# One weight sum of each seven-product pair made by an accumulating DMA, in a hybrid encoder block on one core

## The chip, the cores and the metric

The kernel runs on one core of a Trainium2 chip. The metric is the device time of one execution in microseconds (us). The engines are TensorE (PE; its weight loads are listed as PEld), VectorE (DVE), ScalarE (ACT), GpSimd (POOL) and SyncE (SP). SP issues the loads of the weights; GpSimd issues a few DMAs of its own.

## What is computed

One layer of a streaming encoder: a joint input projection, retention heads, latent-attention heads, an output projection, a layer norm, and a feed-forward part. The change lies in the feed-forward part, on 256 tokens:

```
x = LN(alpha * x + concat(A, B) @ W_out)          # 256 x 2048
h = square(relu(x @ W_up)) @ W_down               # W_up 2048 x 8192, W_down 8192 x 2048
x = LN(alpha * x + h)
```

All of it is float32.

## The kernel before, in words

**Products in parts.** TensorE multiplies in a rounded form of float32 (fp32r). To keep the precision, every operand is split into a high part (rounded, a ScalarE cast, L389) and a low part (operand minus high part, a VectorE subtraction, L390), and every product is three matmuls: high by high, high by low, low by high. Tokens are the stationary operand, weights the moving one, 512 columns at a time.

**Pairs.** The weights come in pairs of 128-row slices: a load of 1 MB fills a raw tile of 128 x 2048 that holds two slices of 1024 columns each. Call the slices' column halves B11, B12 (first slice) and B21, B22 (second slice), and the four token blocks of the activations x11 to x22 alike. An ordinary pair (pair_products, L1293) splits each slice once (two splits of 1024 columns, two slots) and runs 24 matmuls. A seven-product pair, or seven (seven_products, L429), uses Winograd's form of Strassen's scheme: seven products of 128 x 128 by 128 x 512 in place of eight, 21 matmuls. It needs four sums of the token blocks (token_sums, L360: four VectorE instructions L364 to L367, a ScalarE cast L368 and a VectorE subtraction L369 for the low part) and, of the weights, three sums made on VectorE in weights_pair (L371): t13 (1024 columns, L398), a new content of B12 in place (512 columns, L404), and t4 (512 columns, L408). Four splits follow: w0 (second slice), w1 (first slice), w2 (t13), w3 (t4, 512 columns).

**What sets the order.** Every pair is a Job with a load and a list of pieces. unit(), called after each group of matmuls, hands out up to two pieces (next_piece, L177) in the order of the jobs; SEVEN_PARTS gives the order within a seven: token sums s0, t13 s1, split w0, s2, w2, s3, w1, w3. Split weights live in five slots (NSLOT) of a high and a low tile; a split waits for the slot that was used five splits earlier, while sums need no slot and may be handed out ahead. Raw tiles are three (NRAW): load_ahead (L160) issues the load of a job on SP's queue when the job three ahead of it has been handed out, and on the chip it waits for that job's last reader of the raw tile.

**Up stage.** After a first part with other shapes (j_up), seven blocks b = 1 to 7 run eight pairs each over 1024 columns of W_up. UP_SEVEN makes pairs 3 and 5 of block 1 and pairs 2, 3, 5, 6 of the other six blocks sevens: 26 in all. Their token sums are made once (pair_sums). The products that belong to several outputs gather in four PSUM banks; up_gather (L1309) combines them, up_finish adds them to the block's result, which TensorE transposes.

**Down stage.** Two passes p = 0, 1 over 1024 columns of W_down each; in each pass 32 pairs at places n = 0 to 31. ORDER and TURNED give the order of the pairs, SEVEN the places that are sevens. At every even place r_split splits the next block of activations (ScalarE cast L1233, VectorE low part L1237); in pass 0, r_keep stores the low part in HBM by a GpSimd DMA (L1243), and pass 1 fetches it by a GpSimd DMA (L1235). A seven of pass 1 whose pair is in STORED = (27, 9, 22, 25, 4, 7) uses the token sums that pass 0 left in the tile sx; every other seven makes its own. add_sums (L1394) combines the gathered products after the last seven of a pass, one step per unit; in pass 1 its last step is two matmuls (L1428). The last four pairs of pass 1 are staged, their splits kept for the end. The retention stage has sevens too (half_pair, L454); they go through weights_pair as well.

Of the kernel before, what the change touches and what calls it, by code (L numbers as in the profile page):

```python
# [12 lines left out]
ALU = mybir.AluOpType  # L13

P = 128
# [22 lines left out]
SEVEN = ((4, 7, 9, 12, 14, 17, 19, 22, 25, 27), (2, 4, 6, 8, 10, 12, 14, 16, 18, 20, 22))  # L38
# [5 lines left out]
SEVEN_PARTS = ('s0', 's1', 'w0', 's2', 'w2', 's3', 'w1', 'w3')  # L44
X1_AT = ((1, 2), 1)
# [47 lines left out]
class Job:  # L93


    def __init__(self, load, pieces, slotted):
        self.load = load
        self.pieces = pieces
        self.slotted = slotted
        self.slots = None  # L100
        self.left = None
        self.seven = False
        self.held = False
# [8 lines left out]
def kernel(  # L112
# [45 lines left out]
    state = {"dma": 0, "job": 0, "unit": 0, "pause": 0, "heads": 0}  # L158
# [202 lines left out]
    def token_sums(r0, r1, st, v):  # L361
# [4 lines left out]
        nc.vector.tensor_sub(st[:, 2], r0[:, 0:P], r0[:, P:])  # L366
# [4 lines left out]
    def weights_pair(name, load, half, columns, sums=None, seven=False, into=None):  # L371
# [24 lines left out]
        def first():  # L396
            a, b, t13 = columns(job, extra["t13"])
            nc.vector.tensor_sub(t13, a, b)  # L398
            if sums:
                job.rest()  # L400
# [8 lines left out]

        job.load = lambda: load(job)  # L410
        job.seven = seven
        if not seven:
            job.pieces = [lambda e=e: split(e, half(job, e, 0, 8)) for e in range(2)]
            job.slots = [e if into is None or into[e] is None else None for e in range(2)]
        else:
            parts = {"s0": token_part, "s1": first, "s2": second, "s3": third,
                     "w0": lambda: split(0, half(job, 1, 0, 8)), "w1": lambda: split(1, half(job, 0, 0, 8)),
                     "w2": lambda: split(2, extra["t13"]), "w3": lambda: split(3, extra["t4"], 512)}
            job.pieces = [parts[p] for p in SEVEN_PARTS]
            job.slots = [int(p[1]) if p[0] == "w" else None for p in SEVEN_PARTS]  # L420
# [8 lines left out]
    def seven_products(job, x, k, sums, cb, mb, first, last, done=None):  # L429
        for a, w, o, pb, alone in ((("x", 1, 0), 0, 0, cb[0][0], False), (("s", 3), 0, 512, cb[0][1], False),  # L430
                                   (("s", 0), 2, 0, mb[2], True), (("s", 2), 2, 512, mb[3], True),
                                   (("x", 0, 0), 1, 0, mb[0], True), (("s", 1), 1, 512, mb[1], True),
                                   (("x", 1, 1), 3, 0, cb[1][0], False)):
# [110 lines left out]
    def up_pair(b, kp):  # L544
        def load(job):
            raw = raw_tile(job, f"raw_wu{b}_{kp}")
            nc.sync.dma_start(raw.rearrange("p (f c) -> p f c", f=8),
                              w_up[8 * b:8 * b + 8, :, kp * 256:(kp + 1) * 256].rearrange("f p c -> p f c"))

# [3 lines left out]
        def columns(job, t):  # L553
            v = job.raw.rearrange("p (f e c) -> p f e c", f=8, e=2)
            return (v[:, 4:8].rearrange("p f e c -> p e f c"), v[:, :, 0].rearrange("p (j f) c -> p j f c", j=2),
                    t.rearrange("p (j f c) -> p j f c", j=2, c=P))

        return weights_pair(f"wu{b}_{kp}", load, half, columns, None, kp in UP_SEVEN[b])

    def down_pair(p, pair, into=None, seven=None):  # L560
        def load(job):
            raw = raw_tile(job, f"raw_wd{p}_{pair}")
            nc.sync.dma_start(raw.rearrange("p (e c) -> p e c", e=2),
                              w_down[2 * pair:2 * pair + 2, :, p * 1024:(p + 1) * 1024].rearrange("e p c -> p e c"))

# [9 lines left out]
        def columns(job, t):  # L575
            return (job.raw.rearrange("p (e j c) -> p e j c", e=2, j=2)[:, :, 1],
                    job.raw[:, 0:1024].rearrange("p (j c) -> p j c", j=2), t.rearrange("p (j c) -> p j c", j=2))

        return weights_pair(f"wd{p}_{pair}", load, half, columns, None if seven is None or p == 1 and pair in STORED else sums, seven is not None, into)
# [729 lines left out]
    def up_gather(mb):  # L1309
# [10 lines left out]
        nc.vector.tensor_add(g[1], g[1], g[3])  # L1320
        yield
        nc.vector.tensor_add(g[3], g[3], g[2])
# [73 lines left out]
    def add_sums(p, mb):  # L1396
# [14 lines left out]
        nc.vector.tensor_add(v, v, p5)  # L1411
        yield
        plus(1, 1, v)
        nc.vector.tensor_add(u, u, p5)
# [195 lines left out]
```

## Time and profile before

| | |
|---|---|
| median of 3 runs | 1100.75 us (1100.7 to 1100.85) |
| the profiled execution | 1100.88 us |
| its span, first to last instruction | 1099.1 us |
| granted TensorE clock | 0.999 |
| POOL busy | 24.7 us, 46 instructions |
| DMA | 231.78 MB, mean 211 GB/s |
| up blocks 1 to 7 / down passes, in the span | to about 754 us / to about 1090 us |

The span is what the profiler records from the first to the last instruction; the time of the execution has 1.8 us more around it. A row of instructions reads: start in us, duration, engine, line, operation, destination <- sources, shapes, count, and in brackets the idle time before it with what ended it. A row grouped by line ends in: busy us in total, mean ns of one, idle us before them. A DMA row gives the size of one transfer and the median time from its issue to its landing. "PE d L353" is a matmul into a tile called d issued from line 353, the line of the ordinary pairs; L441 is that of the sevens.

### The profile page before, as it was taken

What the parts mean: (1) busy time and instruction counts of PE and PEld (TensorE: products, weight loads), DVE (VectorE), ACT (ScalarE), POOL (GpSimd) and SP (SyncE); (2) the same over time, 40 slices, a digit from 0 to 9 for tenths busy, and PEclk for the clock granted to TensorE, in tenths of its full rate; (3) what the DMA queues carried; (4) which work ended last, traced back from release to release, by engine and by line L of the source; (5) the groups of instructions that cost most, each with busy time, mean ns of one, the idle gap of its engine ahead of it and who ended that gap; (6) DMA issues with size and microseconds to landing.
All of it is one profiled execution on the core that took longest, in us unless ns stands there. A gap on an engine that the chain in (4) does not pass through costs nothing.

```text
span 1099.1 us, 13768 instructions
## 1 busy us (share of the span) xinstructions
PE 1091.1 (99%) x5145; PEld 912.1 (83%) x5145; DVE 955.4 (87%) x1304; ACT 656.7 (60%) x847; POOL 24.7 (2%) x46
## 2 busy tenths in 40 slices
PE   9999999999999999999999999999999999999997
PEld 8888888888888889888888888888888888888885
DVE  7878779889785777889999999999899999999985
ACT  4545556546463455467777677776666663666660
POOL 0000000000000000000000000000000000000000
PEclk9999999999999999999999999999999999999999
DMA  8655364535266544666656756757677876777792
GB/s 286 243 201 188 138 225 171 222 115 208 109 230 230 216 176 154 194 200 197 213 171 196 234 165 192 230 181 271 205 249 253 260 239 220 264 238 263 255 336 97
DMA packets 97026, 231.78 MB, mean 211 GB/s; under 512 B 4672, under 2 KB 63040, under 8 KB 89152
## 3 DMA queue, kind: packets, MB, share of 16 engines
q1 hardware_dynamic: 92496, 215.64, 57.6%
q0 software_dynamic: 4032, 14.68, 3.9%
q8 instruction: 40, 0.66, 0.2%
q10 hardware_dynamic: 432, 0.59, 0.2%
q14 instruction: 26, 0.21, 0.1%
HBM read 221.46 MB, written 9.44 MB: 210 GB/s over the span
## 4 chain that ended last, share of the span: by engine, by line
PE 97%; DVE 1%; DMA 1%; issue 0%; ACT 0%; POOL 0%; SPq 0%; DVEq 0%
PE d L353 21%; PE u L353 15%; PE r L353 12%; PE o L353 8%; PE v L441 6%; PE s L441 5%; PE u L441 5%; PE m L353 5%; PE d L441 4%; PE rs L441 2%; PE up L924 2%; PE pu L924 2%; PE r L441 1%; PE ut L1353 1%; PE pv L353 1%; PE up L930 1%
## 5 line engine op out<-in xcount | busy, mean ns | idle before, releaser
L353 PE MATMUL d<-hi_wd,rhl 128*128 128x512 f32 x632 | 174.7, 390 | 0.0
L390 DVE TENSOR_TENSOR lo_wd<-raw_wd,hi_wd 128x1024 fp32r<-128x1024 f32 x125 | 150.4, 1220 | 19.9 <-ACT hi_wd L389 19.5
L389 ACT CAST hi_wd<-raw_wd 128x1024 fp32r<-128x1024 f32 x125 | 129.3, 1051 | 56.1 <-DVE raw_wd L404 17.8
L390 DVE TENSOR_TENSOR lo_wu<-raw_wu,hi_wu 128x1024 fp32r<-128x1024 f32 x112 | 135.5, 1220 | 12.0 <-ACT hi_wu L389 10.9
L353 PEld LDWEIGHTS d<-hi_wd,rhl 128*128 128x128 f32 x632 | 118.4, 188 | 24.3
L389 ACT CAST hi_wu<-raw_wu 128x1024 fp32r<-128x1024 f32 x112 | 117.7, 1055 | 34.5 <-PE u L353 10.6
L353 PE MATMUL u<-hi_wu,x1hl 128*128 128x512 f32 x480 | 137.0, 394 | 0.0
L353 PE MATMUL r<-hi_ret,xhl 128*128 128x512 f32 x384 | 110.2, 397 | 0.0
L353 PEld LDWEIGHTS u<-hi_wu,x1hl 128*128 128x128 f32 x480 | 88.3, 188 | 17.2
L353 PE MATMUL d<-lo_wd,rhl 128*128 128x512 f32 x316 | 97.7, 389 | 0.0
L353 PEld LDWEIGHTS r<-hi_ret,xhl 128*128 128x128 f32 x384 | 71.0, 188 | 14.1
L390 DVE TENSOR_TENSOR lo_ret<-raw_ret,hi_ret 128x1024 fp32r<-128x1024 f32 x64 | 76.1, 1218 | 6.9 <-ACT hi_ret L389 6.7
L389 ACT CAST hi_ret<-raw_ret 128x1024 fp32r<-128x1024 f32 x64 | 65.9, 1052 | 25.6 <-PE r L353 14.7
L353 PE MATMUL u<-lo_wu,x1hl 128*128 128x512 f32 x240 | 74.2, 390 | 0.0
L353 PEld LDWEIGHTS d<-lo_wd,rhl 128*128 128x128 f32 x316 | 59.3, 188 | 12.4
L353 PE MATMUL r<-lo_ret,xhl 128*128 128x512 f32 x192 | 59.5, 391 | 0.0
L353 PE MATMUL o<-hi_wo,mix 128*128 128x512 f32 x208 | 57.5, 393 | 0.0
L441 PE MATMUL v<-hi_wu,us 128*128 128x512 f32 x156 | 56.5, 389 | 0.0
L353 PEld LDWEIGHTS u<-lo_wu,x1hl 128*128 128x128 f32 x240 | 45.0, 188 | 9.6
L441 PE MATMUL s<-hi_wd,sx 128*128 128x512 f32 x126 | 45.6, 389 | 0.0
L353 PEld LDWEIGHTS o<-hi_wo,mix 128*128 128x128 f32 x208 | 38.7, 188 | 7.8
L240 ACT CAST hi_wo<-raw_wo 128x1024 fp32r<-128x1024 f32 x26 | 27.0, 1054 | 27.4 <-PE o L353 19.1
(341 smaller groups left out, 2210.6 us busy)
## 6 DMA issues: line engine op xcount, KB each, us to landing
raw_wu<-in_w_up SPq DMA_DIRECT2D x64, 1024.0 KB, 5.4
raw_wd<-in_w_down SPq DMA_DIRECT2D x64, 1024.0 KB, 5.9
raw_ret<-in_w_ret SPq DMA_DIRECT2D x32, 1024.0 KB, 4.8
raw_wo<-in_w_out SPq DMA_DIRECT2D x16, 1024.0 KB, 4.8
raw_mla<-in_w_mla SPq DMA_DIRECT2D x14, 672.0 KB, 5.1
lo_kept<-rhl POOLq DMA_DIRECT2D x14, 512.0 KB, 4.1
rhl<-lo_kept POOLq DMA_DIRECT2D x13, 512.0 KB, 3.6
raw_qk<-in_w_qk SPq DMA_DIRECT2D x8, 640.0 KB, 3.9
```

Of the source, the lines that this page charges most:

```text
L240: nc.scalar.copy(hi[:, o:e], r)
L353: nc.tensor.matmul(accs[j][:, :w], x_part, w_part[:, a:a + w], start=first and fst and i == 0, stop=last and lst and i == len(steps) - 1)
L389: nc.scalar.copy(h, src)
L390: nc.vector.tensor_sub(l, src, h.bitcast(F32))
L441: nc.tensor.matmul(pb, x_part, w_part, start=alone and first and fst, stop=alone and last and lst)
L924: nc.tensor.matmul(pb, hi[:, a:a + P], hl[:, k0 + i], start=first and i == ks[0], stop=last and i == ks[-1])
L930: nc.tensor.matmul(pb[:, 0:S], lo[:, a:a + P], hl[:, k0 + i, 0:S], start=False, stop=last and i == ks[-1])
L1353: nc.tensor.transpose(pts[i][:, f * P:(f + 1) * P], gathered[i][:, f * P:(f + 1) * P], ident)
```

## The change

In the up and down stages (not in retention), a seven is made in a new way. After the load of its raw tile, GpSimd issues a DMA that reads the first half of the first slice (B11) from HBM once more and adds it to the second half (B12) in the raw tile: 512 rows of 512 bytes in the up stage, 128 rows of 2 KB in the down stage, 256 KB each. add_ahead issues it, from next_piece, once the job before it is being handed out. VectorE then makes t4 = (B11 + B12) - B22 (512 columns) and t13 = [B11, B21] - t4 (1024 columns, t4 read twice). The order within a seven becomes s0, s2, s3, w0, w1, w2, w3 (ADDED_PARTS), the low part of the token sums follows t4, and the seven products run in another order over the four splits. Some sums have the opposite sign, so the third token sum and the combinations in up_gather and add_sums change signs. The places of the sevens in the down passes become 4, 6, 8, 11, 13, 16, 18, 21, 23, 25, 27 (eleven, ten before) and 3, 5, ..., 23 (eleven, as before at 2, 4, ..., 22). STORED, TURNED, UP_SEVEN, NRAW and NSLOT stay as they are.

```diff
-SEVEN = ((4, 7, 9, 12, 14, 17, 19, 22, 25, 27), (2, 4, 6, 8, 10, 12, 14, 16, 18, 20, 22))
+SEVEN = ((4, 6, 8, 11, 13, 16, 18, 21, 23, 25, 27), (3, 5, 7, 9, 11, 13, 15, 17, 19, 21, 23))
...
 SEVEN_PARTS = ('s0', 's1', 'w0', 's2', 'w2', 's3', 'w1', 'w3')
+ADDED_PARTS = ('s0', 's2', 's3', 'w0', 'w1', 'w2', 'w3')
...
+    def add_ahead():
+        while state["added"] and jobs.index(state["added"][0][0]) <= state["job"] + 1:
+            _, dst, src = state["added"].pop(0)
+            nc.gpsimd.dma_start(dst, src, accum_op=ALU.add)
...
         load_ahead(state["job"])
+        add_ahead()
...
-        nc.vector.tensor_sub(st[:, 2], r0[:, 0:P], r0[:, P:])
+        nc.vector.tensor_sub(st[:, 2], r0[:, P:], r0[:, 0:P])
...
             nc.vector.tensor_sub(t13, a, b)
-            if sums:
-                job.rest()
...
+        def added_second():
+            b22 = half(job, 1, 4, 8)
+            nc.vector.tensor_sub(shaped(extra["t4"], b22), half(job, 0, 4, 8), b22)
+            if sums:
+                job.rest()
+
+        def added_third():
+            low = columns(job)
+            t4, t13 = extra["t4"], extra["t13"].rearrange("p (e c) -> p e c", e=2)
...
+            nc.vector.tensor_sub(t13, low, t4.unsqueeze(1).to_broadcast(low.shape))
...
+        if job.plus:
+            steps = ((("x", 1, 0), 0, 0, cb[0][0], False), (("s", 3), 0, 512, cb[0][1], False),
+                     (("x", 0, 0), 1, 0, mb[0], True), (("s", 0), 1, 512, mb[2], True),
+                     (("s", 2), 2, 0, mb[3], True), (("x", 1, 1), 2, 512, cb[1][0], False),
+                     (("s", 1), 3, 0, mb[1], True))
...
-                if done and w == 1:
+                if done and w == (3 if job.plus else 1):
                     side.append(done)
...
+            if job.seven:
+                state["added"].append((job, half(job, 0, 4, 8),
+                                       w_up[8 * b:8 * b + 4, :, kp * 256:kp * 256 + P].rearrange("f p c -> p f c")))
...
+            if job.seven:
+                state["added"].append((job, raw[:, 512:1024], w_down[2 * pair, :, p * 1024:p * 1024 + 512]))
...
-        nc.vector.tensor_add(g[1], g[1], g[3])
+        nc.vector.tensor_sub(g[1], g[3], g[1])
...
-        nc.vector.tensor_add(v, v, p5)
+        nc.vector.tensor_sub(v, p5, v)
```

More of the change, by code (lines that the diff above doesn't have):

```diff
@@ L102, in __init__ @@
         self.seven = False
+        self.plus = False
         self.held = False
@@ L157 @@
     holders = []
-    state = {"dma": 0, "job": 0, "unit": 0, "pause": 0, "heads": 0}
+    state = {"dma": 0, "job": 0, "unit": 0, "pause": 0, "heads": 0, "added": []}
     def load_ahead(upto):
@@ L369, in token_sums, with weights_pair @@
         return lambda: nc.vector.tensor_sub(v[:, :, 1], st, v[:, :, 0].bitcast(F32))
-    def weights_pair(name, load, half, columns, sums=None, seven=False, into=None):
+    def weights_pair(name, load, half, columns, sums=None, seven=False, into=None, plus=False):
         job = Job(None, [], into is None or None in into)
@@ L408, in third @@
             nc.vector.tensor_sub(shaped(extra["t4"], b21), b21, half(job, 0, 4, 8))
+        def added_second():
[6 more added lines that the diff above has]
+            t4, t13 = extra["t4"], extra["t13"].rearrange("p (e c) -> p e c", e=2)
+            if len(low.shape) == 4:
+                t4 = t4.rearrange("p (f c) -> p f c", c=P)
+                t13 = t13.rearrange("p e (f c) -> p e f c", c=P)
+            nc.vector.tensor_sub(t13, low, t4.unsqueeze(1).to_broadcast(low.shape))
         job.load = lambda: load(job)
         job.seven = seven
+        job.plus = plus
         if not seven:
@@ L415, in weights_pair @@
         else:
-            parts = {"s0": token_part, "s1": first, "s2": second, "s3": third,
+            parts = {"s0": token_part, "s1": first, "s2": added_second if plus else second,
+                     "s3": added_third if plus else third,
                      "w0": lambda: split(0, half(job, 1, 0, 8)), "w1": lambda: split(1, half(job, 0, 0, 8)),
                      "w2": lambda: split(2, extra["t13"]), "w3": lambda: split(3, extra["t4"], 512)}
-            job.pieces = [parts[p] for p in SEVEN_PARTS]
-            job.slots = [int(p[1]) if p[0] == "w" else None for p in SEVEN_PARTS]
+            names = ADDED_PARTS if plus else SEVEN_PARTS
+            job.pieces = [parts[p] for p in names]
+            job.slots = [int(p[1]) if p[0] == "w" else None for p in names]
         job.hi, job.lo = [None] * 4, [None] * 4
@@ L429, in seven_products @@
     def seven_products(job, x, k, sums, cb, mb, first, last, done=None):
[L430 to L433, printed above, removed]
+        if job.plus:
[3 more added lines that the diff above has]
+                     (("s", 1), 3, 0, mb[1], True))
+        else:
+            steps = ((("x", 1, 0), 0, 0, cb[0][0], False), (("s", 3), 0, 512, cb[0][1], False),
+                     (("s", 0), 2, 0, mb[2], True), (("s", 2), 2, 512, mb[3], True),
+                     (("x", 0, 0), 1, 0, mb[0], True), (("s", 1), 1, 512, mb[1], True),
+                     (("x", 1, 1), 3, 0, cb[1][0], False))
+        for a, w, o, pb, alone in steps:
             use_slot(job, w)
@@ L548, in load, with columns @@
                               w_up[8 * b:8 * b + 8, :, kp * 256:(kp + 1) * 256].rearrange("f p c -> p f c"))
+            if job.seven:
+                state["added"].append((job, half(job, 0, 4, 8),
+                                       w_up[8 * b:8 * b + 4, :, kp * 256:kp * 256 + P].rearrange("f p c -> p f c")))
         def half(job, e, i, j):
             return job.raw.rearrange("p (f e c) -> p f e c", f=8, e=2)[:, i:j, e]
[L553 to L558, printed above, removed]
+        def columns(job):
+            return job.raw.rearrange("p (f e c) -> p f e c", f=8, e=2)[:, 0:4].rearrange("p f e c -> p e f c")
+        return weights_pair(f"wu{b}_{kp}", load, half, columns, None, kp in UP_SEVEN[b], plus=True)
     def down_pair(p, pair, into=None, seven=None):
@@ L573, in sums, with columns @@
             return token_sums(r0, r1, st, sums_of(seven, pair))
[L575 to L579, printed above, removed]
+        def columns(job):
+            return job.raw.rearrange("p (e j c) -> p e j c", e=2, j=2)[:, :, 0]
+        return weights_pair(f"wd{p}_{pair}", load, half, columns, None if seven is None or p == 1 and pair in STORED else sums, seven is not None, into, True)
     def sums_of(q, pair):
```

4 lines of the change are left out of this document (2 added, 2 removed).

## The prediction, on record before the result

> **What bounds the kernel now.** I read the page's busy table first, then the chain of waits with its steps in order of time, then who waits for whom on the engine that carries the chain, and only then the stages.
>
> ```profile
> span 1099.1 us, 13768 instructions
> PE 1091.1 (99%) x5145; PEld 912.1 (83%) x5145; DVE 955.4 (87%) x1304; ACT 656.7 (60%) x847; POOL 24.7 (2%) x46
> ...
> PE 97%; DVE 1%; DMA 1%; issue 0%; ACT 0%; POOL 0%; SPq 0%; DVEq 0%
> ```
>
> A busy share of 99% alone proves little, since the ends of matmuls are modelled. The chain says more: 97% of the span is TensorE following itself. The next rows are the chain in order of time inside the second down pass, one ordinary pair and one seven-product pair ("a seven" from here on).
>
> ```profile
> 938.83 5.44 PE d L353 x24
> 944.27 1.36 PE d L441 x6
> 945.63 2.72 PE s L441 x12
> 948.35 0.68 PE d L441 x3
> ```
>
> A pair is 24 matmuls in 5.44 us, 226.7 ns each. A seven is 21 in 1.36 + 2.72 + 0.68 = 4.76 us, the same 226.7 ns each. So neither contains a wait. The list of TensorE's waits agrees; these are its two longest entries (us in total, times, longest), one at the start of the kernel and one in its tail:
>
> ```profile
> PE last L1513 <- ACT xm L1511: 1.5, 1, 1.5
> PE m L616 <- POOL warm L613: 1.0, 1, 1.0
> ```
>
> TensorE is therefore fed everywhere in the up and down stages, and time falls only by removing matmuls. The stages show how narrowly it is fed (columns: TensorE, weight loads, VectorE, ScalarE, GpSimd, clock, DMA share, GB/s):
>
> ```profile
> 600.00:700.00 100.00, 100.00 (x458) 82.80 (x458) 94.82 (x104) 73.04 (x90) 0.00 (x0) 1.00 0.63 199
> 800.00:900.00 100.00, 100.00 (x443) 82.84 (x442) 97.76 (x123) 64.90 (x73) 4.78 (x9) 1.00 0.75 246
> 900.00:1000.00 100.00, 100.00 (x442) 82.68 (x442) 94.20 (x111) 59.48 (x65) 3.72 (x7) 1.00 0.72 249
> ```
>
> VectorE is at 95 to 98% there. It is not the bound, but it is next, and whatever stalls it has little room.
>
> **The change, part by part.**
>
> *Matmuls.* The first down pass gets 11 sevens for 10; the second keeps 11, the up blocks 26. One pair becomes a seven: 5.44 - 4.76 = 0.68 us less on the path. The new order of the seven steps keeps 21 matmuls each and costs nothing on TensorE, as long as the operands are there.
>
> *VectorE, removed and added.* Durations of one, by line and form:
>
> ```profile
> L404 DVE TENSOR_TENSOR raw_wu<-raw_wu,t 128x512 f32<-128x512 f32 x26 | 17.9, 688 | 0.4
> L404 DVE TENSOR_TENSOR raw_wd<-raw_wd,t 128x512 f32<-128x512 f32 x21 | 14.4, 684 | 0.0
> L364 DVE TENSOR_TENSOR xm<-rr 128x128 f32<-128x128 f32 x15 | 4.3, 284 | 0.0
> L369 DVE TENSOR_TENSOR sx<-xm,sx 128x512 fp32r<-128x512 f32 x15 | 10.3, 684 | 0.0
> ```
>
> Consecutive instructions overlap a little, so I count from start to start, from this piece of the first down pass (last split of a pair, then a seven):
>
> ```profile
> 861.12 1.22 DVE L390 TENSOR_TENSOR lo_wd<-raw_wd,hi_wd 128x1024 fp32r<-128x1024 f32 x1
> 862.26 0.28 DVE L364 TENSOR_TENSOR xm<-rr 128x128 f32<-128x128 f32 x1
> ...
> 863.19 1.22 DVE L398 TENSOR_TENSOR t<-raw_wd 128x1024 f32<-128x1024 f32 x1
> 864.33 0.69 DVE L369 TENSOR_TENSOR sx<-xm,sx 128x512 fp32r<-128x512 f32 x1
> 864.93 1.22 DVE L390 TENSOR_TENSOR lo_wd<-raw_wd,hi_wd 128x1024 fp32r<-128x1024 f32 x1
> ```
>
> A 1024-wide instruction takes 1.14 us, a 512-wide one 0.60, the four token sums 0.93. Per seven, three weight instructions (1024, 512, 512) become two (512, 1024): the L404 one goes, 26 + 21 = 47 times 0.60 = 28.2 us. The eleventh seven costs 0.60 + 1.14 + 3 x 1.14 + 0.60 = 5.76 us of weight work where a pair has 2 x 1.14 = 2.28: plus 3.5. And there is a part that the title doesn't name. The second pass reuses six token sums of the first through the list STORED (pairs 27, 9, 22, 25, 4, 7), which the change leaves alone; its sevens move to odd places, that is to pairs 31, 23, 24, 26, 1, 3, 5, 6, 8, 11, 13, and none of them is in the list. So the second pass makes 11 sets of sums for 5, the first 11 for 10: 22 sets for the 15 of the rows above, 7 x (0.93 + 0.60) = 10.7 us more. Sum on VectorE: -28.2 + 3.5 + 10.7 = -14 us, all beside TensorE's work: worth nothing by itself. ScalarE gets seven more 512-wide casts and about 1.7 us for the new seven, under its 40% of idle time: nothing.
>
> *The sums by DMA.* 48 transfers of 256 KB from HBM, each added into the upper half of a weight tile in SBUF. Each waits on GpSimd's queue for the tile's own load to land; the first VectorE weight instruction of the seven, and ScalarE's cast for the second split, wait for the sum. What has to fit is load plus sum into the cover between the issue of the load and that VectorE instruction. No accumulating transfer is in this trace. Its neighbours (KB each, us to landing; then GpSimd's time for one descriptor job):
>
> ```profile
> raw_wu<-in_w_up SPq DMA_DIRECT2D x64, 1024.0 KB, 5.4
> raw_wd<-in_w_down SPq DMA_DIRECT2D x64, 1024.0 KB, 5.9
> lo_kept<-rhl POOLq DMA_DIRECT2D x14, 512.0 KB, 4.1
> rhl<-lo_kept POOLq DMA_DIRECT2D x13, 512.0 KB, 3.6
> out<-xm SPq DMA_DIRECT2D x6, 256.0 KB, 2.2
> ```
>
> ```profile
> L1243 POOL DMA_DIRECT2D lo_kept<-rhl x14 | 7.7, 547 | 469.2 <-PE u L353 344.3 <-DVE rhl L1237 124.9
> ```
>
> Low end: the 256 KB store, 2.2 us; a gain is excluded, since the transfer is added. High end: two 1 MB loads and a store that overlapped,
>
> ```profile
> raw_wd<-in_w_down SPq DMA_DIRECT2D x2, 1024.0 KB, 8.3
> ```
>
> landed 2.4 us later than the median load, so 4.1 + 2.4 = 6.5 us; in the up blocks a sum has 512 rows of 512 bytes for the 128 rows of the GpSimd row, and if that job grows fourfold from 0.547 us, 1.6 us more: 8.1. I take 3.9, the middle of the two GpSimd rows of 512 KB, because a sum moves 256 KB in and has to read and write 256 KB at its target. Load plus sum is then 9.3 us in the up blocks and 9.8 in the down passes.
>
> The Trainium skill (page Collectives: The Full Stack, section "The bandwidth ceiling: the fold count and why AG ≠ RS ≠ AR") says that an adding transfer runs at about half a copy's rate, not for the addition but because it reads two sources. By that rule a 256 KB sum costs what a 512 KB copy costs here; were it a mere copy, 2.2 us, load plus sum would be 7.6 and 8.1 us and no seven would be late. No row here shows an adding transfer, so neither is tested yet.
>
> *The cover.* Issues of the load that feeds a seven, and the instruction that will need the sum (the sevens of an up block, then of the first pass after two pairs, then of the second pass):
>
> ```profile
> 619.56 0.37 SPq L547 DMA_DIRECT2D raw_wu<-in_w_up  x1
> 628.85 1.22 DVE L398 TENSOR_TENSOR t<-raw_wu 128x1024 f32<-128x1024 f32 x1
> 856.09 0.37 SPq L563 DMA_DIRECT2D raw_wd<-in_w_down  x1
> 958.79 0.37 SPq L563 DMA_DIRECT2D raw_wd<-in_w_down  x1
> 968.88 0.28 DVE L364 TENSOR_TENSOR xm<-rr 128x128 f32<-128x128 f32 x1
> 979.87 0.28 DVE L364 TENSOR_TENSOR xm<-rr 128x128 f32<-128x128 f32 x1
> ```
>
> Up: 628.85 - 619.56 = 9.3 us, even with 9.3. First pass: 863.19 - 856.09 = 7.1; there the tile is freed by a seven's third split, and in the new order by its second, 1.14 us earlier, so 8.2 against 9.8: 1.6 us late, at the three sevens that follow two pairs. At the seven other steps, with one pair between, the load goes out at the end of the pair ahead of the seven before, and the cover is 0.93 plus a whole step of 10.7 us (below). Second pass: 968.88 + 0.93 - 958.79 = 11.0, 1.2 to spare.
>
> *Does VectorE bear the lateness?* A seven with token sums takes it 5.76 + 0.93 + 0.60 = 7.29 us. First pass, seven and pair: 7.29 + 2.28 + 1.14 (the low part of the next block's activations) = 10.71 against TensorE's 10.20, -0.5; with two pairs 7.29 + 4.56 + 1.7 = 13.6 against 15.6, +2.1, and +0.5 after the 1.6 us. Over its ten steps (places 4, 6, 8, 11, 13, 16, 18, 21, 23, 25, 27), 7 x -0.5 + 3 x 0.5 = -2. The lead that pays for it is thin now; the tightest place of this pass is the pair at
>
> ```profile
> 857.72 3.49 DVE L390 TENSOR_TENSOR lo_wd<-raw_wd,hi_wd 128x1024 fp32r<-128x1024 f32 x3
> 859.87 10.88 PE d L353 x48
> ```
>
> whose first split ends at 857.72 + 1.22 = 858.94, 0.9 us ahead of TensorE. Each seven before it now gives 0.60 back, so some 2 us of lead stand against the -2: just enough. Second pass: 7.29 + 2.28 = 9.6 against 10.2, lead grows. So nothing of the lateness reaches TensorE, by a small margin.
>
> *What else is moved.* GpSimd's queue also stores and fetches the kept low parts; a store behind a waiting sum has two blocks (20 us) until its buffer is rewritten, a fetch one block (10.2 us) for its 3.6: hidden unless a sum waits over 6 us. The combination of partial products after the last seven starts one unit later, and its two matmuls in the second pass then fall in the last unit of place 27, ahead of the staged pairs: nothing.
>
> Total: -0.68 us. The profiled execution took 1100.88 (span 1099.1 and 1.8 around it), so 1100.20; against the median of the runs, 1100.75, it is 1100.1.
>
> **Rivals.**
>
> *The sums land late* (slower). They share the 16 DMA engines with loads that fill 63 to 75% of them; 51 GB/s more in the second pass (256 KB read twice per 10.2 us) is about a sixth more. VectorE works in order, so a late sum stops splits, gathers and residuals alike. In the first pass a seven after two pairs breaks even at 2.1 us late, that is at a sum of 4.4 us, and the lead is gone near 5. In the second pass loads run two steps ahead, the step becomes (load + sum + 9.57 - 0.93)/2, and passes 10.20 at a sum of 5.9. With 6.5 us: first pass 3 x (12.4 - 8.2 + 13.6 - 15.6 = 2.1) + 7 x 0.5 less 3 of lead = 7; second 10 x 0.3 less 2 to 3 of lead, about 1; together 1108. With 8.1 the same sums give 12 and 9, 1121, and the up blocks, 4.2 us late at their first seven, come on top. For it: VectorE at 97.8%, the 8.3 us row. Against: the 3.6 and 4.1 rows were made beside that same traffic. The Trainium skill (page DMA: Bandwidth & Descriptors, section "Issuing engines are not separate DMA queues") states that transfers from any engine interleave on the same 16. The 8.3 us row agrees.
>
> *The second pass pays for its sums* (slower). Its steps with sums now take 979.87 - 968.88 = 10.99 us, with waits for ScalarE inside, such as
>
> ```profile
> 978.73 1.23 DVE L390 TENSOR_TENSOR lo_wd<-raw_wd,hi_wd 128x1024 fp32r<-128x1024 f32 x1 [0.67 <-ACT hi_wd L389]
> ```
>
> Less 0.60 that is 10.4, and if the token sums' own cast on ScalarE, which now has one 0.60 us instruction beside it and not one of 1.14, adds a wait of 0.4 (an estimate), 10.8: 10 x 0.6 less 2 of lead, 1104. Against: this wait stands at a pair's second split because the cast of the activations comes ahead of it, and the odd places move that cast among a seven's splits.
>
> *Faster by over 2.2 us* would need TensorE waits that a freer VectorE ends; the rows show none in these stages.
>
> *A small loss*: lateness as forecast, but a lead somewhere too short, up to 2.9 us: 1100.1 to 1102.9.
>
> **How the numbers follow.** A measurement of this kernel tells 0.2%, 2.2 us, from no change. Forecast as worked, 0.50: 1100.1. Small loss, 0.16; with the forecast that is within 0.2%: 0.66. Late sums 0.24 and the second pass's sums 0.07: slower 0.31. Faster 0.03. The range runs from 1099.6 (the faster case left out) to 1108, the price at 6.5 us; about half of the late case, 0.12, lies above.
>
> **What would show it.** Right: TensorE's chain keeps 5.44 and 4.76 us per pair and seven to the end; L404 gone from these tiles; 22 rows of L364; accumulating transfers landing in 3 to 5 us; VectorE waiting on them 1 to 2 us at first-pass sevens after two pairs. Wrong: sums landing above 5 us, VectorE's waits on them in the second pass or in every up block, and TensorE waiting for split tiles.

## The result, and the profile after

The changed kernel takes 1148.74 us (median of 4 runs, 1141.51 to 1149.22), the kernel before 1100.72 beside it (1100.61 to 1100.85): a ratio of 1.042, 95% interval 1.038 to 1.046. The prediction was 1100.1, with a range to 1108: wrong, by 48 us. The profiled execution of the changed kernel took 1148.98, its span is 1147.2.

The page, the busy table and the chain's shares:

```profile
span 1147.2 us, 13933 instructions
...
PE 1104.8 (96%) x5142; PEld 912.9 (80%) x5142; DVE 941.4 (82%) x1296; ACT 656.5 (57%) x856; POOL 77.6 (7%) x94
...
PE 43%; DMA 25%; DVE 22%; issue 6%; ACT 3%; POOLq 0%; POOL 0%; DVEq 0%; ACTq 0%
```

The chain was 97% TensorE; now a quarter of it is DMA and a fifth VectorE. VectorE is 14.0 us less busy, as forecast, and the kernel is slower all the same. The stages, from the starts of TensorE's matmuls in each trace (first of up block 1, first of the first down pass, first of the second, last of the second), in us; the times are medians of all executions, the stages those of the one profiled execution. The profiled execution took 1120.9 us for e5 (its four executions: 1121, 1123, 1134 and 1135), 1153.1 for e3, 1162.6 for e9 and 1114.6 for e7; the others lie within 1.2 us of their medians. The rows below the second are the experiments, told further down:

| kernel | time | up blocks | pass 1 | pass 2 |
|---|---|---|---|---|
| before | 1100.7 | 298.3 | 169.2 | 166.9 |
| changed | 1148.7 | 307.0 | 190.5 | 184.9 |
| e1 down sums that nobody waits for | 1113.3 | 312.5 | 168.5 | 166.8 |
| e2 plain copies for sums | 1122.5 | 299.2 | 182.1 | 174.0 |
| e3 split w0 first | 1156.8 | 310.2 | 189.1 | 187.0 |
| e4 kernel before, new places | 1106.0 | 298.3 | 170.2 | 170.0 |
| e5 split loads | 1128.7 | 310.2 | 170.2 | 173.8 |
| e5b split loads, w0 first | 1135.9 | 298.9 | 182.4 | 188.2 |
| e7 quarter sums | 1116.7 | 298.3 | 178.5 | 171.1 |
| e8 kernel before, eleven in pass 1 | 1104.1 | 298.3 | 171.5 | 167.4 |
| e9 sevens at every third pair | 1158.5 | 312.4 | 195.3 | 187.7 |
| e10 split loads, w0 first in up only | 1112.9 | 298.3 | 170.6 | 176.3 |
| e11 plain down loads halved | 1116.9 | 309.3 | 174.3 | 166.8 |
| e12 new algebra, sums on VectorE | 1104.1 | 298.8 | 170.9 | 169.2 |
| e13 sevens at every fifth pair | 1124.1 | 309.6 | 174.1 | 173.4 |
| e14 four sums by DMA | 1104.7 | 298.7 | 171.2 | 167.3 |
| e16 new algebra, old places | 1101.4 | 298.3 | 169.2 | 167.1 |

The loss is 8.7 + 21.3 + 18.0 = 48.0 us: a little in the up blocks, the rest in the two down passes. The up blocks of the same code differ between executions: 307.0 to 312.5 us in the five kernels that have the same up blocks (changed, e1, e9, e11, e13).

What takes the time in the second pass is seen in the chain in order of time, from the load of one seven to the load of the seven after next (start in us, duration, what). Below it, of the waits, the one that VectorE has for the sums and the one that it hands on to TensorE (us in total, times, longest):

```profile
1043.37 6.87 DMA raw_wd<-in_w_down
...
1050.88 7.62 DMA raw_wd<-in_w_down
...
1058.52 0.69 DVE ut L418
1059.21 0.60 DVE sx L377
1059.81 1.14 DVE t L428
1060.94 2.69 DVE lo_wd L398 x3
1063.64 0.63 issue
1064.27 2.95 DVE lo_wd L398 x3
...
1067.25 7.23 DMA raw_wd<-in_w_down
```

```profile
DVE ut L418 <- DMA raw_wd<-in_w_down: 52.4, 18, 6.3
...
PE d L471 <- DVE lo_wd L398: 26.3, 17, 4.4
```

A load of 1 MB (6.87 us), 0.64 us until GpSimd's transfer is out, the sum (7.62), then VectorE's work on the seven and on the pair behind it (8.7 us), and only then is the raw tile of that pair free, into which the load of the seven after next goes. TensorE is not in it at all. The piece takes 1067.25 - 1043.37 = 23.9 us and holds two pairs and two sevens, for which TensorE needs 20.4. 3.5 us lost per two steps, five times, is 17.5 of the 18.0.

Landings by group, medians (KB each, us from issue to landing), and the queue that carries GpSimd's transfers (packets, MB, share of 16 engines):

```profile
raw_wu<-in_w_up SPq DMA_DIRECT2D x64, 1024.0 KB, 5.8
raw_wd<-in_w_down SPq DMA_DIRECT2D x64, 1024.0 KB, 6.8
...
lo_kept<-rhl POOLq DMA_DIRECT2D x14, 512.0 KB, 7.0
raw_wu<-in_w_up POOLq DMA_DIRECT2D x26, 256.0 KB, 5.7
rhl<-lo_kept POOLq DMA_DIRECT2D x13, 512.0 KB, 5.8
raw_wd<-in_w_down POOLq DMA_DIRECT2D x22, 256.0 KB, 7.2
```

```profile
q0 software_dynamic: 20928, 27.27, 11.5%
```

The sums land in 5.7 and 7.2 us, not in 3.9, and what runs beside them lands later: a down load 6.8 for 5.9, a store of the kept low parts 7.0 for 4.1. (Their fetch takes 5.8 for 3.6 too, but that need not be the sums' doing: it takes 6.4 in e16, which has no sum by DMA.)

Not all sums are so slow. Two short stretches of the same pass, the transfers issued in each:

```profile
raw_wd<-in_w_down POOLq DMA_DIRECT2D x1, 256.0 KB, 3.5
```

```profile
raw_wd<-in_w_down SPq DMA_DIRECT2D x2, 1024.0 KB, 7.4
rhl<-lo_kept POOLq DMA_DIRECT2D x1, 512.0 KB, 6.3
raw_wd<-in_w_down POOLq DMA_DIRECT2D x1, 256.0 KB, 7.6
```

The first (966 to 969 us) is a sum issued when no load was in flight: 3.5 us. The second (1050 to 1057) is the sum of the chain above, with two loads and a fetch issued around it: 7.6. Over all 22 down sums, from issue and landing of each transfer in the trace: the 16 that had on average 1.8 or more other transfers in flight took 7.3 us on average (4.2 to 8.6); the three that had at most 1.2 took 3.5 to 3.8. In the up blocks it is the moment that divides them: the eleven sums with a load issued within 1 us of their own issue took 6.4 to 7.9 us, the other fifteen 4.2 to 6.1. In the down passes fourteen of sixteen such sums took 6.5 to 8.6, the other two 4.4 and 5.0. The Trainium skill (page DMA: Bandwidth & Descriptors, section "Queues, rings and completion order") has each of the 16 engines take turns between the queues, one whole packet from each; these rows agree in that transfers of different queues slow each other, and don't show the turns.

### The profile page after: what moved, and what is told of

It reads as the page before. It is cut to its first block, busy times and chain, and to the rows that moved or that the text cites. A ratio compares the mean times of both kernels' runs of the same rounds, so it can differ in the third digit from the quotient of the medians.

```text
span 1147.2 us, 13933 instructions
## 1 busy us (share of the span) xinstructions
PE 1104.8 (96%) x5142; PEld 912.9 (80%) x5142; DVE 941.4 (82%) x1296; ACT 656.5 (57%) x856; POOL 77.6 (7%) x94
## 3 DMA queue, kind: packets, MB, share of 16 engines
q0 software_dynamic: 20928, 27.27, 11.5%
## 4 chain that ended last, share of the span: by engine, by line
PE 43%; DMA 25%; DVE 22%; issue 6%; ACT 3%; POOLq 0%; POOL 0%; DVEq 0%; ACTq 0%
DMA raw_wd<-in_w_down 14%; PE r L361 11%; DMA raw_wu<-in_w_up 11%; DVE lo_wd L398 7%; PE o L361 7%; DVE lo_wu L398 5%; PE m L361 4%; DVE t L428 3%; PE d L361 3%; PE rs L471 2%; DVE ut L418 2%; PE u L361 2%; PE pu L956 2%; PE r L471 1%; DVE rhl L1269 1%
## 5 line engine op out<-in xcount | busy, mean ns | idle before, releaser
L361 PE MATMUL d<-hi_wd,rhl 128*128 128x512 f32 x616 | 171.0, 390 | 0.9 <-ACT rhl L1265 0.9
L397 ACT CAST hi_wd<-raw_wd 128x1024 fp32r<-128x1024 f32 x125 | 128.3, 1050 | 58.1 <-DMA raw_wd<-in_w_down 37.6
L398 DVE TENSOR_TENSOR lo_wd<-raw_wd,hi_wd 128x1024 fp32r<-128x1024 f32 x125 | 147.6, 1218 | 8.1 <-ACT hi_wd L397 8.0
L398 DVE TENSOR_TENSOR lo_wu<-raw_wu,hi_wu 128x1024 fp32r<-128x1024 f32 x112 | 132.5, 1218 | 6.3 <-ACT hi_wu L397 6.3
L361 PEld LDWEIGHTS d<-hi_wd,rhl 128*128 128x128 f32 x616 | 115.3, 188 | 25.3 <-ACT rhl L1265 1.3
L418 DVE TENSOR_TENSOR ut<-raw_wd 128x512 f32<-128x512 f32 x22 | 15.2, 691 | 52.4 <-DMA raw_wd<-in_w_down 52.4
L175 POOL DMA_DIRECT2D raw_wu<-in_w_up x26 | 33.6, 1293 | 302.3 <-DVE lo_wu L398 98.7
L376 ACT CAST sx<-xm 128x512 fp32r<-128x512 f32 x22 | 13.7, 621 | 68.7 <-DVE xm L375 68.7
```

Source lines behind the costliest of these rows:

```text
L175: nc.gpsimd.dma_start(dst, src, accum_op=ALU.add)
L361: nc.tensor.matmul(accs[j][:, :w], x_part, w_part[:, a:a + w], start=first and fst and i == 0, stop=last and lst and i == len(steps) - 1)
L376: nc.scalar.copy(v[:, :, 0], st)
L397: nc.scalar.copy(h, src)
L398: nc.vector.tensor_sub(l, src, h.bitcast(F32))
L418: nc.vector.tensor_sub(shaped(extra["t4"], b22), half(job, 0, 4, 8), b22)
```

## The experiments

Theory 1: a chain of latencies through the three raw tiles, as above. Theory 2: traffic, the accumulating transfers slow every load. Theory 3: the second pass's eleven token sums computed anew.

**e1: nobody waits for the down sums.**

```diff
-            _, dst, src = state["added"].pop(0)
+            job, dst, src = state["added"].pop(0)
+            if dst is None:
+                dst = scratch
+                nc.gpsimd.tensor_copy(scratch[:, 0:1], job.raw[:, 512:513])
...
-                state["added"].append((job, raw[:, 512:1024], w_down[2 * pair, :, p * 1024:p * 1024 + 512]))
+                state["added"].append((job, None, w_down[2 * pair, :, p * 1024:p * 1024 + 512]))
```

> The changed kernel, but each of the 22 sums of the down passes goes into a scratch tile that no instruction reads, started by a one-column copy on GpSimd when the pair's load has landed: the same DMAs over the same bytes, and VectorE waits for the load alone (what is left out: the sum B12 + B11 in the down projection). Theory 1, a chain of latencies (load, then sum, then the seven's VectorE work, then the next load into one of the three raw tiles): the chain loses its 7.2 us of sum, the second pass goes back to its 10.2 us a step, the 39 us that the down passes lost go to under 5, and the time is 1107 to 1114 (up still pays its 9). Theory 2, traffic (what the accumulating transfers take of the 16 engines slows every load): the transfers are all still there, so the time stays above 1135. Theory 3, the eleven token sums that pass 2 computes anew: also stays, above 1135.

Measured 1113.28 us, ratio 1.0108 (1.0094 to 1.0121). The transfers are there and nearly as slow as in the changed kernel:

```profile
raw_wd<-in_w_down SPq DMA_DIRECT2D x64, 1024.0 KB, 6.6
...
scratch<-in_w_down POOLq DMA_DIRECT2D x22, 256.0 KB, 6.7
```

The down passes take 168.5 + 166.8 = 335.3 us, 0.8 less than before: the 0.68 us of three matmuls, and nothing else. So all of the 39 us there is waiting for sums. Theory 2 falls as a cost by itself, theory 3 falls for the changed kernel. What is left is the up blocks, which were not touched.

**e2: plain copies** (`accum_op=ALU.add` left off).

> The changed kernel with plain copies on GpSimd's queue where it has accumulating ones: the same bytes written, at the same places and with the same waits, only without the add (what is left out: the sum, B12 is written over by B11). Theory 1: what counts is how long the second transfer takes. A plain 256 KB should land in 4 to 5 us where the accumulating one took 7.2 in the down passes, so load and copy make 11 to 12 us and the step (11.5 + 8.64)/2 = 10.1, at the edge of 10.2: 1102 to 1115. Theory 2: half of the added load on the 16 engines goes, so about half of the loss stays: 1118 to 1130. Theory 3: no change, above 1140.

Measured 1122.48, ratio 1.0202 (1.0186 to 1.0217): the number of theory 2, not of theory 1. The copies landed faster, but in the down passes not by what I had assumed:

```profile
q0 software_dynamic: 7872, 27.27, 7.3%
...
raw_wu<-in_w_up POOLq DMA_DIRECT2D x26, 256.0 KB, 4.2
```

In the down passes they took 5.5 us in the median. In the up blocks 4.2 us was enough, nearly all of the 9 us went; the down passes kept 20. With e1, traffic matters, but through the landings that stand in the chain. The queue's shares also give a price. The kernel before has 3.9% of 1099.1 = 42.9 us there, e2 7.3% of 1119.9 = 81.8, the changed kernel 11.5% of 1147.2 = 131.9: per transfer 0.81 us of all 16 engines for a copy of 256 KB and 1.85 for a sum, 2.3 times as much. The rule of the Trainium skill that the prediction cited (page Collectives: The Full Stack, section "The bandwidth ceiling: the fold count and why AG ≠ RS ≠ AR": an adding transfer at about half a copy's rate) agrees with that in size. Its reason, the second read, isn't shown here: the copies also go in far fewer packets (7872 on this queue for 20928), and no run sets the two apart. Nor does the rule say how long a sum takes to land among others.

**e4 and e8: the new places alone, the eleventh seven alone** (the kernel before with one constant changed; e8 has SEVEN[0] = (4, 7, 9, 11, 14, 16, 18, 20, 22, 25, 27) and the old second pass).

> The kernel before with the new places of the sevens (eleven in the first down pass, the odd places in the second), and its own VectorE sums and signs: no GpSimd DMA. It sets apart what the new places cost: pass 2 finds none of its sevens among the stored token sums and computes eleven anew, on VectorE. Theory 1 and theory 2 expect little: 1099 to 1106. Theory 3 expects most of the 48 us here: above 1130.

> The kernel before with eleven sevens in the first down pass at places (4, 7, 9, 11, 14, 16, 18, 20, 22, 25, 27): all ten of the stored pairs' and other places' token sums as before, the second pass untouched, VectorE sums, no GpSimd DMA. It leaves nothing out and takes three matmuls away, 0.68 us, for about 5.4 us more VectorE work in the first pass (one more token sum set and the pair's own sums). If VectorE has that to spare there: 1099.9 to 1100.7. If the stretch from place 9 to 22 is VectorE-bound: 1101 to 1106.

e4: 1106.01, ratio 1.0044 (1.0032 to 1.0057), at the upper edge of what theories 1 and 2 expected and far from theory 3. e8: 1104.08, ratio 1.0029 (1.0018 to 1.0040), in the range for a stretch that VectorE binds. An eleventh seven made on VectorE takes 0.68 us of matmuls away and costs 3 us net. The windows from 850 to 875 us, before and e8 (length, then TensorE, weight loads, VectorE, ScalarE, GpSimd, clock, DMA share, GB/s):

```profile
850.00:875.00 25.00, 25.00 (x112) 20.72 (x111) 24.49 (x29) 17.88 (x21) 1.49 (x3) 1.00 0.78 261
```

```profile
850.00:875.00 25.00, 24.49 (x101) 18.00 (x100) 24.93 (x33) 15.60 (x18) 1.06 (x2) 1.00 0.72 233
```

VectorE was at 98% and is now at 99.7%, and TensorE waits. In e4 the second pass, which makes eleven sets of token sums for five, takes 3.1 us more. Without the waits for sums, the changed kernel, where VectorE has 0.60 us less per seven, pays neither (e1).

**e5, e3 and e5b: two ways to shorten the chain.** e5 brings a seven's load in three transfers, the 256 KB that the sum goes to first; e3 puts the split w0, which needs no sum, ahead of the wait; e5b does both.

```diff
-            nc.sync.dma_start(raw.rearrange("p (e c) -> p e c", e=2),
-                              w_down[2 * pair:2 * pair + 2, :, p * 1024:(p + 1) * 1024].rearrange("e p c -> p e c"))
...
+                for e, i, j in ((0, 512, 1024), (0, 0, 512), (1, 0, 1024)):
+                    nc.sync.dma_start(raw[:, e * 1024 + i:e * 1024 + j], w_down[2 * pair + e, :, p * 1024 + i:p * 1024 + j])
```

```diff
-ADDED_PARTS = ('s0', 's2', 's3', 'w0', 'w1', 'w2', 'w3')
+ADDED_PARTS = ('s0', 'w0', 's2', 's3', 'w1', 'w2', 'w3')
```

> The changed kernel, but a seven's 1 MB load comes as three transfers on SP's queue, the 256 KB that the sum is added to first (then the other 256 KB of that half of the pair, then the last 512 KB). Nothing is left out, and as many bytes move. Theory 1: the sum can start some 2 to 4 us earlier, beside the rest of its own load, and the chain of two steps (23.9 us) loses that: 21 to 22 us for two steps, or 10.5 to 11, so 1112 to 1130. If the chain closes (under 10.2 a step) 1102 to 1110. Theory 2: the bytes are the same, so no change or slightly worse by the smaller transfers: above 1143.

> The changed kernel with one change of order: in a seven's VectorE work the split of B21 and B22 (w0), which needs only the load, stands ahead of the subtraction that waits for the sum (and, in the down passes, ahead of the token sums' last step). Nothing is left out. Theory 1, the chain of latencies: ScalarE's copy and VectorE's subtraction of that split (some 2.4 us) then lie inside the wait for the sum and no longer behind it, so the raw tile comes free 2.4 us earlier per seven and two steps of the second pass take 23.9 - 2.4 = 21.5 us, 10.75 a step: of the down passes' 39 us some 12 to 17 stay, and of the 9 in the up projection 0 to 5: 1113 to 1126. Theory 2 (the accumulating transfers slow every load; half of the loss stayed with plain copies): as many transfers and bytes, above 1140.

> Split loads (the 256 KB that the sum is added to first) and the split of B21 and B22 ahead of the wait, both. Nothing is left out. With the split load alone the down passes lost 7.9 us and the up projection 11.7. Theory 1: the down passes' chain closes (another 2.4 us off two steps puts it under 10.2 a step), leaving 0 to 4 us there, most of it what the new places cost (4 us); the up projection gets 2.4 us a seven shorter and keeps 2 to 8: 1103 to 1113. Theory 2: no gain over the split load alone, 1125 to 1135.

e5: 1128.68, ratio 1.0247 (1.0197 to 1.0298): the median is where theory 1 had it, but two of the four executions (1134 and 1135 us) lie above its 1130. In the profiled one, the fastest of the four, the down passes got back 31 of their 39 us; where the slower two lost their 14 us more no trace shows. The up blocks got nothing back: their sums, now beside the rest of their own loads, landed later,

```profile
raw_wu<-in_w_up POOLq DMA_DIRECT2D x26, 256.0 KB, 7.6
...
raw_wd<-in_w_down POOLq DMA_DIRECT2D x22, 256.0 KB, 4.5
```

e3: 1156.8, ratio 1.0504 (1.0487 to 1.0521), slower than the change itself: a miss for theory 1, and above 1140 as theory 2 had it, but not for its reason. The wait for the sums is nearly gone (11.6 us in the down passes, for 52.4), and two others have come:

```profile
ACT hi_wd L397 <- DVE t L428: 47.6, 21, 2.8
...
DVE lo_wd L398 <- ACT hi_wd L397: 45.4, 43, 4.4
```

With w0 first, ScalarE no longer casts it while VectorE makes t4 and t13. The two engines take turns, as in this seven of the second pass (VectorE's rows, then ScalarE's; idle time before in brackets):

```profile
1050.13 1.23 DVE L398 TENSOR_TENSOR lo_wd<-raw_wd,hi_wd 128x1024 fp32r<-128x1024 f32 x1 [1.64 <-ACT hi_wd L397]
```

```profile
1053.80 1.04 ACT L397 CAST hi_wd<-t 128x1024 fp32r<-128x1024 f32 x1 [2.42 <-DVE t L428]
```

VectorE stands 1.64 us for the cast of w0, and ScalarE then 2.42 us for t13, while neither engine waits more than 0.23 us for a DMA in this seven. e5b: 1135.89, ratio 1.0318 (1.0304 to 1.0332), a miss for theory 1 and 0.9 us above theory 2's range: in the up blocks, where there are no token sums between, both edits together take the loss away (298.9 us), in the down passes they are worse than split loads alone.

**e7: a quarter of each sum** (64 KB).

> The changed kernel with only a quarter of each sum: 64 KB instead of 256 KB, with the same number of accumulating DMAs, at the same places, with the same waits (what is left out: three quarters of B12 + B11). It sets a cost by the byte apart from a cost by the transfer. If the cost goes by the byte, the sum lands in some 3 us instead of 5.7 and 7.2, load and sum make (6.3 + 3 + 8.64)/2 = 9.0 a step, under 10.2, and what is left is the new places' 4 us: 1101 to 1109. If it goes by the transfer (queueing, issue, the semaphore's way), the sum still takes 5 us or more and above half of the loss stays: above 1118.

Measured 1116.69, ratio 1.0141 (1.0127 to 1.0155), between the two expectations.

```profile
raw_wu<-in_w_up POOLq DMA_DIRECT2D x26, 64.0 KB, 3.7
raw_wd<-in_w_down POOLq DMA_DIRECT2D x22, 64.0 KB, 5.2
```

A quarter of the bytes took three quarters of the time in the down passes. By these two medians most of a sum's landing there is not its bytes. The chain of its second pass shows 6.44 + 0.63 + 5.55 + 8.75 = 21.4 us for two steps, still over 20.4.

**e11: smaller loads beside the sums.**

```diff
+            if job.seven:
...
+            else:
+                nc.sync.dma_start(raw[:, 0:1024], w_down[2 * pair, :, p * 1024:(p + 1) * 1024])
```

> The changed kernel with a plain down pair's load cut to one half (512 KB for 1 MB; what is left out: both halves of the pair are then taken from the first, so the down products of those pairs are not the reference's). The sums, their bytes, places and waits are untouched; what shrinks is the transfer that starts in the same moment as a sum. If the sum is slow because it shares the engines with that load (it landed in 3.5 us where nothing else was in flight and in 7.3 with two other transfers), it lands in 4 to 5.5 here, the seven's load in 5.5 to 6.3, and two steps take 5.9 + 0.6 + 4.8 + 8.7 = 20.0 us, under 20.4: down keeps 0 to 8 of its 39 us and the time is 1110 to 1121. If an accumulating transfer takes its 7 us by itself: two steps 21.8 us, 1125 to 1133.

Measured 1116.85, ratio 1.0142 (1.0129 to 1.0156), as expected of sharing.

```profile
raw_wd<-in_w_down SPq DMA_DIRECT2D x22, 1024.0 KB, 5.9
raw_wd<-in_w_down SPq DMA_DIRECT2D x42, 512.0 KB, 3.5
...
raw_wd<-in_w_down POOLq DMA_DIRECT2D x22, 256.0 KB, 5.0
```

The sums are the same, only their neighbours are smaller, and they land in 5.0 us for 7.2. The second pass is back at 166.8. So the slow landing comes from the transfers beside the sum, shown by a run and not only by the order of events.

**e9 and e13: sevens farther apart.**

> The changed kernel with the down sevens at every third pair in place of every other: places (4, 7, 10, 13, 16, 19, 22, 25) and (3, 6, 9, 12, 15, 19, 22), 15 sevens for 22. Nothing is left out; 7 x 0.68 = 4.8 us of matmuls come back. Theory 1, the chain through three raw tiles: a seven's tile is then freed by the seven before it, two plain pairs lie between, and load + sum + VectorE's work (24 us) stand against three steps of 10.2 = 30.7: the chain closes, the down passes cost 4.8 us of matmuls and 0 to 4 more, the up projection keeps its 9 to 14: 1114 to 1124. Theory 2 (each accumulating transfer costs its share of the 16 engines): two thirds of the sums, two thirds of the down passes' 39 us, 26 + 4.8 + 9: 1138 to 1145. From the measured quiet and loaded landings (3.5 and 7.3 us) I also expect shorter landings here, under 6 us in the median.

> The changed kernel with the down sevens at every fifth pair: places (4, 9, 14, 19, 24) and (3, 9, 14, 19), 9 sevens for 22. Nothing is left out; 13 x 0.68 = 8.8 us of matmuls come back. The chain law: a seven's tile is freed by the pair three places earlier. At every third place that is the seven before, so load 6.3 + issue 0.6 + sum 7.5 + the seven's own VectorE work 4.7 = 19.1 us stood against 2 x 5.44 + 4.76 = 15.6 us of matmuls, 3.4 a seven, which is what was measured there. At every fifth, load, sum, the seven and two plain pairs on VectorE, 6.3 + 0.6 + 7.2 + 11.2 = 25.3 us, stand against 4 x 5.44 + 4.76 = 26.5: it closes. The down passes take 336 + 8.2 to 336 + 14 = 344 to 350 us, the up projection 307 to 313 as before, in all 1118 to 1130. If every accumulating transfer cost its 1.8 us of the down passes' 39 by itself: 9 x 1.8 + 8.2 = 24, 360 us for the down passes, 1133 or more.

e9: 1158.45, ratio 1.0509 (1.0468 to 1.055): a miss for both theories and for the shorter landings (7.6 us in the median, not under 6). The mistake was mine: 10.2 us is TensorE's time for a pair and a seven, not for one pair; three pairs with one seven are 15.6 us, not 30.7. At every third place a seven's raw tile is freed by the seven before it:

```profile
1000.14 6.24 DMA raw_wd<-in_w_down
...
1006.95 7.51 DMA raw_wd<-in_w_down
...
1014.48 0.69 DVE ut L418
1015.17 0.60 DVE sx L377
1015.78 1.14 DVE t L428
1016.91 2.28 DVE lo_wd L398 x2
...
1019.21 5.46 DMA raw_wd<-in_w_down
```

19.1 us from load to load against 15.6: some 3.4 us a seven. With e1's passes as the base and 0.68 us for each seven fewer, the two passes lost 195.3 - 170.5 = 24.8 and 187.7 - 169.5 = 18.2 us over 8 and 7 sevens, 3.1 and 2.6 each. e13 tested the law with its arithmetic put right, at the first spacing that I worked out to close: 1124.06, ratio 1.0208 (1.0194 to 1.0222), and 174.1 + 173.4 = 347.5 us for the down passes, inside the 344 to 350 expected; 360 would have been a cost by transfer.

**e12 and e16: the algebra without the DMA.** In both a VectorE `tensor_add` of B11 into B12 stands at the head of the seven's work; e16 has the old places as well.

> The changed kernel with its algebra, signs, product order and places, but the sum B12 + B11 made in place by a VectorE addition at the head of the seven's work (0.60 us) and no accumulating DMA. Nothing is left out. If all that was lost beyond the new places comes from where the sum is made, this equals the kernel before at the new places, 1104.5 to 1107.5 (that one took 1106.0). If the turned signs, the product order or the order of the splits cost something of their own: above 1110.

> The new algebra with the sum made by VectorE at the old places (ten and eleven, the second pass using stored token sums again), no accumulating DMA. Nothing is left out: the same matmuls and as many VectorE operations as the kernel before. Expected the same as before, 1100.3 to 1101.6. If the turned signs or the new order of the splits cost something, above 1102.5, and then that is part of the loss.

e12: 1104.05, ratio 1.0032 (1.0019 to 1.0045), 0.45 us under its range. e16: 1101.36, ratio 1.0002 (0.9994 to 1.0011), as expected. Signs, product order and order of the splits cost nothing; the new places cost 3 us (e12) to 5 us (e4) where VectorE makes the sums.

**e10 and e14: looking for a version that pays.** e10 takes split loads everywhere and w0 first in the up blocks alone. e14 is e16 with eleven sevens in pass 1, four of them summed by DMA.

> All sums by DMA, split loads everywhere, and the split of B21 and B22 ahead of the wait in the up projection alone (there that order gave 298.9 us from block 1 to the first down matmul, against 298.3 before), the other order in the down passes (170.2 and 173.8 us against 169.2 and 166.9). Nothing is left out. If the stages add up: 0.6 + 1.0 + 6.9 = 8.5 us over the kernel before, 1108 to 1111. If the up projection's earlier end only moves the wait (its last loads and the first down pass share the raw tiles): 1114 to 1120.

> The new algebra with VectorE's addition everywhere, the old places in the second pass (its stored token sums used again), eleven sevens in the first at (4, 7, 9, 11, 14, 16, 18, 20, 22, 25, 27), and only four sums by accumulating DMA, at 9, 14, 18 and 22 with split loads. Nothing is left out. By the chain law these four have room (a split load's quarter 3.5 + sum 4.5 = 8 us, against two pairs of matmuls or more), and VectorE is spared 4 x 0.60 us in the stretch where eleven sevens made it late (2.9 us over the kernel before). If that is what binds: 1100.0 to 1102.0, at best 0.7 under the kernel before. If not: 1103 to 1105.

e10: 1112.93 (1110.18 to 1115.44), ratio 1.0111 (1.0092 to 1.0129), between its two expectations; it is the fastest kernel here that keeps all sums by DMA. The up blocks (298.3) and pass 1 (170.6) came as added up, pass 2 (176.3) 2.5 us worse. e14: 1104.69, ratio 1.0035 (1.0023 to 1.0047), as its second expectation had it: four additions fewer on VectorE moved pass 1 only from 171.5 (e8) to 171.2 us, and VectorE is still busy for 98.5 to 99.4% of the 25 us windows from 800 to 925 us. No run beat the kernel before.

## Why the prediction was wrong

*Matmuls: right.* 0.68 us less was forecast, and 0.8 less is what the down passes show once nobody waits (e1).

*VectorE: right.* -14 us forecast, 955.4 to 941.4 measured, worth nothing by itself, as said.

*The sums by DMA: the step that failed.* "I take 3.9" came from medians of GpSimd transfers that run at any time of a pass. A sum runs at one moment only: its load has just landed, other loads are often going out, and it shares the engines with them. Alone it does land in 3.5 us, so the figure was right for a moment that hardly comes. The trace before the change had the sign: of the 13 fetches behind the 3.6 us, the three issued 0.2 to 0.6 us after a load took 6.2 to 6.8 us, seven others 3.4 to 3.6, and the last three lie between. In e16, which has no sum by DMA and another order of the work, that same group has another median:

```profile
rhl<-lo_kept POOLq DMA_DIRECT2D x13, 512.0 KB, 6.4
```

In place of the 3.9 us, 5.7 and 7.2 were measured; the high bound of 6.5 us, from the single row of overlapping loads, was too low for the down passes. The same step took the load as unchanged at 5.9; it became 6.8. And 0.5 to 0.6 us between the load's landing and the start of the transfer was not in the sum. Load plus sum was 9.8 us in the prediction and is 6.8 + 0.6 + 7.2 = 14.6, against a cover of 11.0 in the second pass and of 0.93 + 10.7 = 11.6 at the first pass's steps with one pair between. The case "were it a mere copy", with no seven late, did not come either: the copies of e2 took 5.5 us in the down passes, not 2.2, and 20 us were lost there.

*The lead of some 2 us*: it could pay for 1.6 us once in a while. At 3.5 us lost in every two steps it is gone after one or two.

*"The sums land late": the mechanism that came, with its own formula.* (7.2 + 6.8 + 8.64) / 2 = 11.3 us a step, 11.6 with the gap, and 23.9 / 2 = 12.0 measured. It got 0.24, and against it stood that the neighbours' rows "were made beside that same traffic"; they were, but most of them not at that moment. (The 51 GB/s more are a fifth of the 249 shown, not a sixth.) Its price for the first pass (7 to 12 us) was too small, since I applied the formula to the second pass only: 21.3 us were lost there. Some 4.4 us of these (1.6 and 2.8) are the clock, below.

*"The second pass pays for its sums"*: it does when VectorE makes all sums (e4, +3.1 us in that pass), and not in the changed kernel, whose VectorE has the time.

*The up blocks*: "even with 9.3" was the warning. 5.8 + 5.7 and the gap are 12 us. A copy that lands in 4.2 us, or a quarter sum in 3.7, closes them (e2, e7).

## What to carry to other kernels

Price a transfer at the moment in which it will run: one that is started by the landing of another runs beside whatever that landing lets go, and the median of a group over the whole span is not its price. Where two transfers stand in series in front of a reader and the buffers are few, write down the loop (first transfer, gap, second, the reader's work until the buffer is free), count the jobs that it spans, and compare it with the busiest engine's time for the same jobs. And a DMA that spares an engine which isn't the bound has nothing to win by that alone; here the one thing that the spared time was to buy, an eleventh seven, is worth 0.68 us.

## What the runs showed of the hardware

*A long wait of TensorE slows the matmuls after it.* A wait in the first pass of the changed kernel (start, duration of the modelled matmul, idle time before in brackets):

```profile
806.58 0.39 PE L471 MATMUL d<-hi_wd,rhl 128*128 128x512 f32 x1
809.56 0.80 PE L471 MATMUL d<-lo_wd,rhl 128*128 128x512 f32 x1 [2.59 <-DVE lo_wd L398]
810.15 0.63 PE L471 MATMUL d<-hi_wd,rhl 128*128 128x512 f32 x1
810.58 0.63 PE L471 MATMUL d<-hi_wd,sx 128*128 128x512 f32 x1
...
812.92 0.40 PE L471 MATMUL s<-hi_wd,sx 128*128 128x512 f32 x1
```

After it the matmuls start 0.43 us apart, after 812.9 again 0.23. In four down-pass traces (the changed kernel, e2, e7, e9) I took every gap of over 1 us beyond the usual distance of two matmuls. Up to 2.57 us, all but two left the next 18 matmuls at their pace, and in those two another wait followed at once; all six of 3.26 us and more cost another 1.8 to 2.9 us; of those at 2.75, 2.90 and 2.94 only the first cost anything, 1.6 us. In the changed kernel's down passes the granted clock stands at half in two stretches: one of 3.4 us that begins within the wait above, and one of 6.8 us that begins within the longest wait, which ends at 861.42 (columns as in the windows of e8; 0.50 is the clock):

```profile
809.20:812.60 3.40, 3.04 (x7) 2.47 (x8) 3.40 (x5) 3.24 (x5) 0.00 (x0) 0.50 0.42 95
860.40:867.20 6.80, 5.78 (x14) 4.53 (x15) 6.80 (x7) 3.31 (x4) 1.68 (x3) 0.50 0.71 192
```

The Trainium skill (page TensorE: Matmul & The Clock Gate, section "Part 1: The HAM clock gate (the "warmup" mystery)") puts the idle window at about 3.4 us, free-running. The lengths of the two stretches, one and two such windows, agree. That the wait before 809.56 was enough does not quite, since by its row TensorE had been idle for 2.59 us only.

*GpSimd's own time for a sum* grows with its rows, but far from in proportion: 1293 ns in the mean for 512 rows of 512 bytes (up blocks), 864 ns for 128 rows of 2 KB (down passes), by the groups of line 175. It is 0.87 us both for a sum that landed in 3.5 us (issued at 966.8) and for the slowest, 8.6 us (at 848.0), so it isn't what sets them apart. The fourfold growth behind the prediction's 8.1 us did not come.

*Left open*: why the up blocks need both the split load and w0 first, when either alone leaves them at 310 us; why pass 2 keeps 6.9 (e5) and 9.4 us (e10) over the kernel before with split loads; and why four additions fewer on VectorE give pass 1 with eleven sevens only 0.3 us.
